# One later slot for the filler work of a hybrid decoder step on one core

## The chip, the cores and the metric

The kernel runs on one core of one Trainium2 chip, in one launch. The metric is the time of an execution on the device in microseconds (us); a median of several runs is compared. The engines are called as in the profile: PE (TensorE, the matmuls), PEld (its weight loads), DVE (VectorE), ACT (ScalarE), POOL (GpSimd) and SP (SyncE, which here only issues DMAs). A small q behind a name (SPq, ACTq) is that engine's sequencer issuing a DMA.

## The reference, cut to what matters

One layer of a decoder trunk, for 1024 prompt tokens and 8 sample tokens that share the weights:

```python
h = rmsnorm(x, norm_gain)
q, k, v, gla_g, a_lr, u, pool_g, xq, xg, merge = split(h @ w_in)
o, S   = gla_chunked(q, k, v, log_sigmoid(a_lr @ w_a2 + b_a) / 16, S0)   # gated linear attention, 4 heads
p      = multiscale_pool(u, history, pool_w, pool_scale)                  # trailing means 2/4/8/16
c      = cross_attn(xq, mem_k, mem_v)                                     # 4 heads, 256 memory rows
b      = [rmsnorm(o) * silu(gla_g), p * silu(pool_g), c * silu(xg)]
merged = sum(sigmoid(merge[n]) * (b[n] @ w_branch[n]) for n in range(3))
y      = rmsnorm(x + merged @ w_out, final_gain)
```

The prompt's memory keys and values are themselves products of the memory rows; the sample tokens have their own cached keys, values, GLA states and pooling rows. All of it is float32 in and out. Outputs are y for both groups, the new keys and values, GLA states and pooling rows.

## The kernel before

**Precision.** A float32 product is made of three fast ones: each operand is split into a high part (`h`, by ACT) and a low part (`l`, by DVE), and PE adds high·high, low·high and high·low. In the profile these three are the lines L242 to L244 (`mm3`), the splits L223 and L224 (`split`), or L226 and L227 where a factor is applied as well (the queries, 1/16).

**The backbone.** The input projection `h @ w_in` is cut into 36 pairs of column blocks. Each pair is made of seven products instead of eight (a Strassen-like scheme; the left operands `a11`, `a12`, `s2`, `s1`, `s3`, `s4`, `a22` of `Pair.operands`), each product runs in two halves of 258 columns, 12 matmuls each. Such a half is called a slot here: 36 × 14 = 504 slots. `prepare` splits the left operands three products ahead, and loads the next pair's weights (`raw`, 512 KB each, two per pair, L296) on ACT's DMA queue right behind one of its splits.

**The filler.** Everything between the projection and the branch products is laid into the slots. `fill` (called once after each slot) advances generators: `cross_steps` (cross-attention) and behind it `gla_steps` (GLA), chained by `mix`; then `pool_steps`. A generator yields a number of units after each step; `Stream.run` runs steps as long as the units done are below 493 · (slot − 28) / 329 for `mix`, so a slot is worth 1.4985 units. `pool_steps` starts once `mix` is over, and has its own rate from slot 357 on. So the yields alone say how many slots of backbone matmuls lie between two steps. The sample tokens' own generators (`cross_sample`, `gla_sample`) are advanced from inside `cross_steps` and `gla_steps`.

**Order.** The kernel writes out PE's and SP's order by hand: PE and SP execute in the order of the code. DVE, ACT and POOL are ordered by a scheduler, which arranges them anew when PE's order changes; each then works strictly in its order. The small psum tiles `pz` of the filler have two buffers, the `px` of the backbone six. The four buffers called `own` (function `V`) hold the sample tokens' data, among them in `gla_sample` two states `s` (L674) and two broadcast value rows `vb` (L1036) at a time.

**The places that the change and the prediction touch.** (Line numbers are those of the kernel before; in the changed kernel those after L861 are one lower.)

- Start of `cross_steps`: `cross_memory(0)` and `cross_queries(0, 0)` split keys and queries (`mkT`, `xqs`/`xq`), `cross_rows(0)` turns the sample queries to rows (PE L753, ACT L755) and stores them, then the first `cross_scores` (`pz<-mkTh,xqsh` and the like).
- `gla_sample`, per head: states are updated in L1042 (ACT) and L1043 (DVE), multiplied on PE in L1060, the result is scaled by its norm in L1069 (ACT) and turned over in L1075 (PE).
- `gla_steps`: gates of the next chunk (PE L919, then a long row of DVE work L903 to L947), `gla_within` (PE L956 to L958, then DVE L959 and the split into `ak`), `gla_recur` (PE `pz<-vsh,ak`).
- First step of `pool_steps` for a group: PE L1139 and L1142, DVE L1145 (`f`) and L1146 (`ds`); second step: loads, window sums and PE L1207, which reads `ds`.

Of the kernel before, what the change touches and what calls it, by code (L numbers as in the profile page):

```python
# [24 lines left out]
NH = 4  # L25
# [22 lines left out]
def trunk_kernel(ctx: ExitStack, tc: tile.TileContext,  # L48
# [185 lines left out]
    def split_in(x, shape, name, scale=None):  # L234

        hi, lo = R(shape, F32R, name + "h"), x.bitcast(F32R)
        split(hi, lo, x, scale)
        return hi, lo
# [447 lines left out]
    def cross_load(h):  # L686
        cross["raw", h] = [loaded(mkv_scr[o][h], [2, DV], "mkv") for o in range(2)]

    def cross_memory(h):
        mk, mv = cross["raw", h]  # L690
        t = PZ()
        for i in range(2):
            for a in range(2):
                nc.tensor.transpose(t[:, i * NM + a * P:i * NM + (a + 1) * P], mk[:, a, i * P:(i + 1) * P], ident)
        cross["mk", h] = split_r(t.rearrange("p (i m) -> p i m", i=2), [2, NM], "mkT")
        cross["mv", h] = split_in(mv, [2, DV], "mvs")

    def cross_fetch(h, c):
        cross["xq", h, c] = loaded(chunk_of(xq_raw[h], c), [2, CT], "xq")

    def cross_queries(h, c):
        cross["q", h, c] = split_in(cross["xq", h, c], [2, CT], "xqs", 1.0 / 16.0)

    def cross_scores(h, c):
        xh, xl = cross["q", h, c]
        mh, ml = cross["mk", h]
        t = PZ()
        for j in range(2):
            for i in range(2):
                cs = slice(j * P, (j + 1) * P)  # L710
                mm3(t[:, j * NM:(j + 1) * NM], xh[:, i, cs], xl[:, i, cs], mh[:, i], ml[:, i], i == 0, i == 1)
        nm = tiny(2, "nm")
        nc.vector.tensor_reduce(nm, t.rearrange("p (j m) -> p j m", j=2), axis=AX.X, op=ALU.max, negate=True)
        p = R([2, NM], name="p")
        sm = tiny(2, "sm")
        for j in range(2):
            act(p[:, j], t[:, j * NM:(j + 1) * NM], AF.Exp, bias=nm[:, j:j + 1], accum_out=sm[:, j:j + 1])
        nc.vector.reciprocal(sm, sm)
        for j in range(2):
            nc.vector.tensor_scalar(p[:, j], p[:, j], sm[:, j:j + 1], None, op0=ALU.mult)  # L720
        cross["p", h, c] = p

    def cross_weights(h, c):
        p = cross["p", h, c]
        t = PZ()
        for a in range(2):
            for j in range(2):
                nc.tensor.transpose(t[:, (2 * a + j) * P:(2 * a + j + 1) * P], p[:, j, a * P:(a + 1) * P], ident)  # L728
        cross["pT", h, c] = split_r(t.rearrange("p (a t) -> p a t", a=2), [2, CT], "pT")
# [105 lines left out]
    def cross_steps():  # L835
        def scores(n):
            cross_scores(n // 4, n % 4)

        def memory(n):
            if n % 4 == 0:  # L840
                cross_memory(n // 4)

        def weights(n):
            cross_weights(n // 4, n % 4)

        def values(n):
            cross_values(n // 4, n % 4)

        samples = chain_of(cross_sample(h) for h in range(NH))
        cross_load(0)  # L850
        cross_fetch(0, 0)
        cross_fetch(0, 1)
        yield 1.5
        cross_memory(0)
        cross_queries(0, 0)
        yield 1.5
        cross_scaled(0)
        cross_rows(0)
        yield 1
        for s in range(16 + 2):  # L860
            if s < 16:  # L861
                scores(s)
                if s == 0:
                    cross_queries(0, 1)
                yield 3
                if 0 < s < 15:
                    cross_queries(*divmod(s + 1, 4))
                if s + 2 < 16:
                    cross_fetch(*divmod(s + 2, 4))
            if s % 4 == 2 and s < 14:  # L870
                cross_load(s // 4 + 1)
            if s == 0:
                cross_keys(0, 0)
                cross_keys(0, 1)
            if s >= 1:
                yield next(samples, 0)
            if 0 <= s - 2:
                values(s - 2)
                yield 1.7
            if s >= 1:  # L880
                yield next(samples, 0)
            if s % 4 == 3 and s < 15:
                memory(s + 1)
                yield 2
            if 0 <= s - 1 < 16:
                weights(s - 1)
                yield 1.7
            for _ in range(3):
                if s >= 1:
                    yield next(samples, 0)  # L890
        yield from samples

    def chain_of(gens):
        for g in gens:
            yield from g
# [122 lines left out]
    def gla_sample(h):  # L1018
# [48 lines left out]
        r = rstd_of(sq, 1.0 / DV)  # L1067
        for i in range(2):
            nc.scalar.activation(os_[:, i], os_[:, i], AF.Copy, scale=r[:, i:i + 1])  # L1069
        yield 1  # L1070
        yield 0.5
        t = PZ()
        for i in range(2):
# [157 lines left out]
    def mix():  # L1231
        yield from cross_steps()
        yield from gla_steps()
# [344 lines left out]
```

## Time and profile before

| | |
|---|---|
| median of 3 runs | 1435.47 us (1434.07 to 1435.5) |
| the profiled execution | 1435.0 us, its span 1433.3 us |
| PE busy | 1413.6 us, 99% of the span |
| DVE busy | 916.5 us, 64% |
| ACT busy | 679.4 us, 47% |
| POOL busy | 220.0 us, 15% |
| chain that ended last | PE 93%, DVE 3%, DMA 2%, ACT 1%, issue 1% |
| mean granted PE clock | 0.998 |

The first table of a profile page gives busy time per engine; the chain of what ended last says on which engine the end of the program hung. Both say PE here, nearly without holes. What is to be read beyond that are the holes: the view of waits lists for each engine who ended its idle times, the timeline shows single instructions with the idle time before them in brackets, and the windows view gives the granted clock of a stretch, 1.00 being 2.4 GHz and 0.50 being 1.2 GHz.

### The profile page before, as it was taken

To read this page: it belongs to the slowest core of one execution; us is meant where nothing else is said; L and a number is where in the kernel's file an instruction comes from. 1 tells how busy PE (TensorE), PEld (TensorE's weight loads), DVE (VectorE), ACT (ScalarE), POOL (GpSimd) and SP (SyncE) were. 2 spreads that over 40 slices of the span, in tenths; PEclk is the share of its full clock that TensorE was granted. 3 is DMA by queue.
4 is the path that set the end of the run, shared out by engine and by line. 5 is a ranking of instruction groups with operands and counts; after the bars stand their busy time and mean duration, and the time that the engine had idled before them with its cause. 6 is when DMAs were issued, how large, how long until landed. Compare 5 with 4: busy or idle time off the path is not lost.

```text
span 1433.3 us, 28230 instructions
## 1 busy us (share of the span) xinstructions
PE 1413.6 (99%) x10689; PEld 1354.0 (94%) x10689; DVE 916.5 (64%) x2123; ACT 679.4 (47%) x1575; POOL 220.0 (15%) x401
## 2 busy tenths in 40 slices
PE   7999999999999999999999999999999999999998
PEld 6899999999999998999999999999999999999876
DVE  6956666766777767867765868775672534554336
ACT  6744544444566655656644545444471422333222
POOL 3212111124432212121221111110010000000000
PEclk9999999999999999999999999999999999999999
DMA  9357575666655554555554546566484687632633
GB/s 332 125 165 230 195 254 163 221 211 169 163 163 156 158 173 141 165 157 160 163 152 153 170 154 193 168 206 205 141 278 144 226 265 257 219 103 84 220 120 116
DMA packets 185812, 259.43 MB, mean 181 GB/s; under 512 B 22460, under 2 KB 136916, under 8 KB 185668
## 3 DMA queue, kind: packets, MB, share of 16 engines
q1 hardware_dynamic: 124188, 146.11, 32.8%
q0 software_dynamic: 23328, 73.56, 14.7%
q10 hardware_dynamic: 38160, 37.95, 9.4%
q8 instruction: 84, 1.38, 0.4%
q14 instruction: 52, 0.43, 0.1%
HBM read 180.47 MB, written 77.56 MB: 180 GB/s over the span
## 4 chain that ended last, share of the span: by engine, by line
PE 93%; DVE 3%; DMA 2%; ACT 1%; issue 1%; DVEq 0%; SPq 0%; ACTq 0%
PE px L242 27%; PE px L243 26%; PE px L244 26%; PE pz L244 3%; PE pz L242 3%; PE pz L243 3%; DMA raw<-in_w_in_dram 2%; PE pz L975 1%; PE pz L408 1%; PE pz L956 1%; PE pz L809 1%; PE pz L958 1%; PE pz L728 0%; PE pz L919 0%; DVE ot L224 0%
## 5 line engine op out<-in xcount | busy, mean ns | idle before, releaser
L243 PE MATMUL px<-bl,wbh 128*128 128x384 f32 (+1 forms) x576 | 184.1, 320 | 0.0
L244 PE MATMUL px<-bh,wbl 128*128 128x384 f32 (+1 forms) x576 | 184.1, 320 | 0.0
L242 PE MATMUL px<-bh,wbh 128*128 128x384 f32 (+1 forms) x576 | 183.7, 319 | 0.0
L558 ACT ACTIVATE r<-px 128x258 f32<-128x258 f32 x240 | 90.4, 377 | 63.4 <-PE px L244 62.9
L242 PEld LDWEIGHTS px<-bh,wbh 128*128 128x128 f32 x576 | 108.4, 188 | 0.0
L243 PEld LDWEIGHTS px<-bl,wbh 128*128 128x128 f32 x576 | 108.2, 188 | 0.0
L244 PEld LDWEIGHTS px<-bh,wbl 128*128 128x128 f32 x576 | 108.2, 188 | 0.0
L242 PE MATMUL px<-o,a11h 128*128 128x258 f32 x320 | 94.0, 294 | 0.0
L242 PE MATMUL px<-ot,s3h 128*128 128x258 f32 x320 | 93.3, 292 | 0.1
L242 PE MATMUL px<-ot,s1h 128*128 128x258 f32 x320 | 93.1, 291 | 0.0
L242 PE MATMUL px<-ot,a22h 128*128 128x258 f32 x320 | 92.9, 290 | 0.0
L242 PE MATMUL px<-o,s4h 128*128 128x258 f32 x320 | 92.5, 289 | 0.2 <-DVE c L640 0.2
L242 PE MATMUL px<-o,a12h 128*128 128x258 f32 x320 | 92.5, 289 | 0.0
L242 PE MATMUL px<-ot,s2h 128*128 128x258 f32 x320 | 92.5, 289 | 0.0
L243 PE MATMUL px<-o,a11h 128*128 128x258 f32 x320 | 91.7, 287 | 0.3 <-DVE o L224 0.3
L244 PE MATMUL px<-o,a11l 128*128 128x258 f32 x320 | 91.1, 285 | 0.0
L243 PE MATMUL px<-ot,s2h 128*128 128x258 f32 x320 | 90.1, 282 | 0.5 <-DVE ot L224 0.5
L243 PE MATMUL px<-ot,a22h 128*128 128x258 f32 x320 | 90.6, 283 | 0.0
L243 PE MATMUL px<-o,a12h 128*128 128x258 f32 x320 | 90.4, 283 | 0.0
L244 PE MATMUL px<-o,a12l 128*128 128x258 f32 x320 | 90.4, 283 | 0.0
L244 PE MATMUL px<-ot,s3l 128*128 128x258 f32 x320 | 90.4, 283 | 0.0
L243 PE MATMUL px<-ot,s1h 128*128 128x258 f32 x320 | 90.3, 282 | 0.0
(471 smaller groups left out, 4626.9 us busy)
## 6 DMA issues: line engine op xcount, KB each, us to landing
raw<-in_w_in_dram ACTq DMA_DIRECT2D x72, 512.0 KB, 4.0
msc<-c POOLq DMA_DIRECT2D x24, 516.0 KB, 4.6
brsc<-c POOLq DMA_DIRECT2D x24, 516.0 KB, 3.8
sig<-msc SPq DMA_DIRECT2D x24, 516.0 KB, 6.2
brr<-brsc SPq DMA_DIRECT2D x48, 256.0 KB, 5.0
wbr<-in_w_branch_dram SPq DMA_DIRECT2D x24, 512.0 KB, 5.5
acc<-sig POOLq DMA_DIRECT2D x16, 516.0 KB, 5.6
acc<-acc SPq DMA_DIRECT2D x16, 516.0 KB, 6.8
```

The source lines that it names most:

```text
L242: nc.tensor.matmul(out, lhsT=lh, rhs=rh, start=start, stop=False, skip_group_check=more)
L243: nc.tensor.matmul(out, lhsT=lh, rhs=rl, start=False, stop=False, skip_group_check=more)
L244: nc.tensor.matmul(out, lhsT=ll, rhs=rh, start=False, stop=stop, skip_group_check=more)
L408: nc.tensor.matmul(t[:, :DV], lhsT=memT[k // 2][:, k % 2, a * P:(a + 1) * P], rhs=raw[k // 2][:, k % 2], start=k == 0, stop=k == NK - 1)
L558: nc.scalar.activation(r, acc[c][:, :QT], AF.Copy)
L809: nc.tensor.matmul(t[32 * j:32 * j + 32, :DV], lhsT=pm[:, a, 4 * i + j, :], rhs=vc[j][:, a, :], start=a == 0, stop=a == 1)
L956: nc.tensor.matmul(t[0:64, 0:P], lhsT=ki[:, 0:64], rhs=qi, start=True, stop=True)
L958: nc.tensor.transpose(t[:, P:2 * P], kt, ident)
L975: nc.tensor.matmul(to, lhsT=kiqi[:, 1, cs], rhs=st, start=False, stop=True)
```

## The change

```diff
@@ cross_steps
         yield 1.5
         cross_scaled(0)
         cross_rows(0)
-        yield 1
+        cross_queries(0, 1)
+        yield 2.5
         for s in range(16 + 2):
             if s < 16:
                 scores(s)
-                if s == 0:
-                    cross_queries(0, 1)
                 yield 3
@@ gla_sample
         for i in range(2):
             nc.scalar.activation(os_[:, i], os_[:, i], AF.Copy, scale=r[:, i:i + 1])
-        yield 1
+        yield 1 if h + 1 < NH else 2.5
         yield 0.5
```

No instruction is added or removed. The split of the second block of queries is issued ahead of the first scores, and 1.5 units more stand behind the rows; 1.5 units more stand behind the scaling of the last head's samples. Counted through the units of the 300 steps of `mix`: the first three stay in their slots (29, 30, 31), the next 295 stand exactly one slot later, and the last two stand two slots later. The first step of `pool_steps` moves from slot 359 to slot 361; its second step was in slot 361 and stays there, and so do all others of the pooling.

Place one is the start of the cross stage. On DVE before (L227 splits a block of queries, L713 takes the maximum of scores, L623 is an eviction of the backbone, L718 and L720 end a softmax):

```order
L224 TENSOR_TENSOR mkv<-mkv,mvsh 128x512
L227 SCALAR_TENSOR_TENSOR xq<-xq,xqsh 128x512
L623 TENSOR_TENSOR c_1519<-px,r_1403 128x258
L305 TENSOR_TENSOR ws<-raw 128x512
L713 TENSOR_REDUCE nm<-pz 128x2
L623 TENSOR_TENSOR c_1519<-px,r_1417 128x258
L718 RECIPROCAL sm<-sm 128x2
L720 TENSOR_SCALAR p<-p,sm 128x256 x2
L227 SCALAR_TENSOR_TENSOR xq<-xq,xqsh 128x512
```

and now:

```order
L224 TENSOR_TENSOR mkv<-mkv,mvsh 128x512
L227 SCALAR_TENSOR_TENSOR xq<-xq,xqsh 128x512
L623 TENSOR_TENSOR c_1519<-px,r_1403 128x258
L227 SCALAR_TENSOR_TENSOR xq<-xq,xqsh 128x512
L623 TENSOR_TENSOR c_1519<-px,r_1417 128x258
L224 TENSOR_TENSOR a11l<-raw,a11h 128x512
L713 TENSOR_REDUCE nm<-pz 128x2
```

The second split has moved from behind the first softmax to ahead of the first maximum. On PE the twelve matmuls of one backbone slot now stand between L753 and the first scores, where nothing stood.

Place two is in GLA, around the third L1060 (head 1, first half of the samples). On PE before (`a22` and `a12` are backbone products):

```order
L242 MATMUL px<-ot_986,a22h 128x258
L243 MATMUL px<-ot_987,a22h 128x258
L244 MATMUL px<-ot_986,a22l 128x258
L1060 MATMUL pz<-s_6915,pm 32x256 x2
L1060 MATMUL pz<-s_6919,pm 32x256 x2
L242 MATMUL px<-o_497,a12h 128x258
```

and now (L1059 is the old L1060):

```order
L242 MATMUL px<-o_501,a12h 128x258
L243 MATMUL px<-o_502,a12h 128x258
L244 MATMUL px<-o_501,a12l 128x258
L1059 MATMUL pz<-s_6932,pm 32x256 x2
L1059 MATMUL pz<-s_6936,pm 32x256 x2
L242 MATMUL px<-o_497,a12h 128x258
```

The states' product stands behind the first half of `a12` instead of ahead of it, as everything of GLA stands one slot later against the backbone. On DVE just behind this place, before (L1043 reads `vb`, `ws<-raw` and `a11l` read backbone weights, L903 to L923 are GLA gates):

```order
L224 TENSOR_TENSOR s3l<-ws,s3h 128x512
L623 TENSOR_TENSOR c_7343<-px,r_7204 128x258
L623 TENSOR_TENSOR c_7343<-px,r_7223 128x258
L1043 SCALAR_TENSOR_TENSOR s_7361<-vb,smp,s_7361 128x256
L224 TENSOR_TENSOR a11l<-raw,a11h 128x512
L903 TENSOR_SCALAR bz<-pz,vec 128x256
L305 TENSOR_TENSOR ws<-raw 128x512
L906 TENSOR_TENSOR bz<-bz 128x256
L1043 SCALAR_TENSOR_TENSOR s_7361<-vb,smp,s_7361 128x256
L923 SCALAR_TENSOR_TENSOR bz<-smask,bz 128x256
```

and now (L1042 is the old L1043, L902, L905 and L922 the old L903, L906 and L923):

```order
L623 TENSOR_TENSOR c_7336<-px,r_7218 128x258
L224 TENSOR_TENSOR a11l<-raw,a11h 128x512
L1042 SCALAR_TENSOR_TENSOR s_7370<-vb,smp,s_7370 128x256
L305 TENSOR_TENSOR ws<-raw 128x512
L1042 SCALAR_TENSOR_TENSOR s_7374<-vb,smp,s_7374 128x256
L902 TENSOR_SCALAR bz<-pz,vec 128x256
L1042 SCALAR_TENSOR_TENSOR s_7374<-vb,smp,s_7374 128x256
L905 TENSOR_TENSOR bz<-bz 128x256
L922 SCALAR_TENSOR_TENSOR bz<-smask,bz 128x256
```

The two backbone instructions `a11l` and `ws<-raw` have moved from behind the first L1043 of the second pair of states to ahead of it.

Place three is the start of the pooling. On PE before (`s3` and `a11` are backbone products):

```order
L244 MATMUL px<-ot_817,s3l 128x258
L1139 MATMUL pz<-sel,hist 128x8 x2
L1142 MATMUL pz<-ident,smp 8x128 x2
L242 MATMUL px<-ot_812,s3h 128x258
L243 MATMUL px<-ot_813,s3h 128x258
```

and now (lines one lower):

```order
L244 MATMUL px<-o_429,a11l 128x258
L1138 MATMUL pz<-sel,hist 128x8 x2
L1141 MATMUL pz<-ident,smp 8x128 x2
L1206 MATMUL pz<-ds,pwr 128x8 x4
L242 MATMUL px<-o_421,a11h 128x258
```

The product that reads `ds` (old L1207) stood 24 backbone matmuls behind L1142 and now stands directly behind it. On DVE the two instructions that make `ds` had an eviction between them before:

```order
L1077 TENSOR_SCALAR brs_120<-pz,vec 128x8 x2
L1145 TENSOR_TENSOR f_10457<-pz,smp 128x16
L640 TENSOR_TENSOR c_10272<-px,r_10437 128x258
L1146 SCALAR_TENSOR_TENSOR ds<-f_10457,smp 128x16
L224 TENSOR_TENSOR a12l<-raw,a12h 128x512
```

and now follow each other:

```order
L1076 TENSOR_SCALAR brs_120<-pz,vec 128x8 x2
L640 TENSOR_TENSOR c_10267<-px,r_10445 128x258
L224 TENSOR_TENSOR a12l<-raw,a12h 128x512
L1144 TENSOR_TENSOR f_10495<-pz,smp 128x16
L1145 SCALAR_TENSOR_TENSOR ds<-f_10495,smp 128x16
```

`a12l` and the eviction stand ahead of both.

## Rows read from the trace of the kernel before

**Rows 1.** Waits of PE, whole run (who ended it: us, times, longest us).

```profile
PE pz L956 <- DVE ak L224: 2.4, 1, 2.4
PE pz L1075 <- ACT os L1069: 1.0, 1, 1.0
...
PE pz L244 <- DVE xq L227: 0.7, 2, 0.5
...
PE pz L242 <- ACT xqsh L226: 0.3, 1, 0.3
```

**Rows 2.** Timeline, start of the cross stage (start us, us, instruction, [idle before]).

```profile
122.12 0.39 PE L753 MATMUL pz<-ident,xsq 128*8 128x128 f32 x2
...
122.81 0.38 PE L242 MATMUL pz<-mkTh,xqsh 128*128 128x256 f32 x1 [0.30 <-ACT xqsh L226]
...
123.05 0.68 DVE L227 SCALAR_TENSOR_TENSOR xq<-xq,xqsh 128x512 fp32r<-128x512 f32 x1
...
123.79 0.38 PE L244 MATMUL pz<-mkTh,xq 128*128 128x256 f32 x1 [0.48 <-DVE xq L227]
```

**Rows 3.** Timeline, last GLA samples and first pooling step.

```profile
738.35 0.28 PE L244 MATMUL px<-ot,s1l 128*128 128x258 f32 x1
...
739.63 0.83 PE L1075 MATMUL pz<-ident,os 128*128 128x128 f32 x4 [1.00 <-ACT os L1069]
...
740.22 0.37 PE L242 MATMUL px<-ot,s3h 128*128 128x258 f32 x1
...
741.76 0.51 PE L1139 MATMUL pz<-sel,hist 120*128 120x8 f32 x4
...
742.13 0.38 PE L1142 MATMUL pz<-ident,smp 128*8 128x128 f32 x2
742.26 0.36 PE L242 MATMUL px<-ot,s3h 128*128 128x258 f32 x1
...
742.55 0.17 DVE L1145 TENSOR_TENSOR f<-pz,smp 128x16 f32<-128x16 f32 x1 [1.68 <-PE pz L1142]
...
742.97 0.17 DVE L1146 SCALAR_TENSOR_TENSOR ds<-f,smp 128x16 f32<-128x16 f32 x1
```

**Rows 4.** Timeline behind the third L1060, up to PE's longest wait.

```profile
523.48 0.38 SPq L1036 DMA_DIRECT2D vb<-vs  x1
523.56 0.39 ACTq L296 DMA_DIRECT2D raw<-in_w_in_dram  x1
...
530.37 0.48 DVE L1043 SCALAR_TENSOR_TENSOR s<-vb,smp,s 128x256 f32<-128x256 f32 x1 [3.37 <-ACT s4h L223]
530.77 0.68 DVE L224 TENSOR_TENSOR a11l<-raw,a11h 128x512 fp32r<-128x512 f32 x1
...
533.03 0.69 DVE L305 TENSOR_TENSOR ws<-raw 128x512 f32<-128x512 f32 x1 [1.18 <-DMA raw<-in_w_in_dram]
...
540.16 0.29 PE L956 MATMUL pz<-kiqi 128*64 128x128 f32 x1 [2.43 <-DVE ak L224]
```

**Rows 5.** DMA issues of 523.4 to 523.9 (count, KB each, us to landing).

```profile
raw<-in_w_in_dram ACTq DMA_DIRECT2D x1, 512.0 KB, 9.4
vb<-vs SPq DMA_DIRECT2D x1, 256.0 KB, 6.8
```

**Rows 6.** DMA issues, whole run (count, KB each, median us).

```profile
raw<-in_w_in_dram ACTq DMA_DIRECT2D x72, 512.0 KB, 4.0
```

**Rows 7.** Windows: stretch, its us, busy of PE, PEld, DVE, ACT, POOL, PEclk.

```profile
540.50:543.90 3.40, 3.40 (x18) 3.37 (x17) 2.12 (x9) 3.27 (x12) 0.00 (x0) 0.50 0.03 5
```

**Rows 8.** Timeline, start of GLA.

```profile
372.23 0.46 SPq L674 DMA_DIRECT2D s<-in_state_gla_dram  x1
...
373.48 0.37 ACTq L296 DMA_DIRECT2D raw<-in_w_in_dram  x1
...
378.42 0.69 DVE L305 TENSOR_TENSOR ws<-raw 128x512 f32<-128x512 f32 x1
...
385.20 0.35 PE L242 MATMUL pz<-vsh,ak 128*128 128x256 f32 x1 [0.24 <-DVE ak L224]
```

## Prediction

> **What bounds the kernel now.** I read the page's busy table and its chain first: PE is busy 99% of the span and carries 93% of the chain, so time can only come out of PE's holes, or out of stretches in which its clock is low. The change neither adds nor removes an instruction; it can only open and close holes. So the next view was the list of who ended PE's waits [rows 1]. Leaving out the first 70 us, which the change does not reach, it is short: one wait of 2.4 us for DVE's split `ak` in GLA, one of 1.0 for the scaling `os` of the last head's samples, and three at the first two score blocks of the cross stage (0.3 for `xqsh`, 0.7 in two waits for `xq`). The timelines of those places came next [rows 2 to 4], then the landing times of the DMAs beside them [rows 5, 6], and last the granted clock behind the longest wait [rows 7]: for 3.4 us behind it PE runs at 0.50, the lower of its two levels, at which it does half of what it would do. The mean of 0.998 over the span leaves 2.9 us lost to the clock in all, of which this stretch is 1.7; a second one like it has no room beside it.
>
> A wait costs a little more than its idle time. At L1075 the start is 1.28 us behind that of the last backbone matmul (738.35 to 739.63) where the usual step is about 0.13 (twelve in 740.22 to 741.76); 1.00 is idle, so 0.15 more is lost when the pipeline starts again [rows 3].
>
> **The change part by part.** The scale is the slot: its twelve matmuls take 1.54 us [rows 3].
>
> *Start of the cross stage.* Before, the first scores follow L753 at once. They stand until ACT has split the queries (0.30) and, at their third matmul, until DVE has made the low part, which ends at 123.05 + 0.68 = 123.73 (0.48) [rows 2]. The remaining 0.2 of the 0.7 is the second block, whose split comes late behind the first softmax. With one slot between, the first scores come at about 122.36 + 1.5 = 123.9 and need the low part 0.25 later, at 124.1, 0.4 behind 123.73. The second block's split is now done ahead of the first maximum, so its wait goes too. The split holds up one eviction of the backbone by 0.6 us on DVE; the six `px` buffers cover that. Together 1.0 of idle time and three restarts of 0.15: −1.4 us. Bounds: −1.4, and 0 if the split still arrives last.
>
> *Scaling of the last samples.* L1075 gets one slot more distance. The scaling came 1.00 late, a slot is 1.54, so the wait goes: −1.15 with its restart. Bounds −1.15 and 0.
>
> *First pooling step.* It moves two slots, the second step none, so L1207 now stands right behind L1142. PE could have gone on at 742.26, the start of its next instruction; instead it must wait for `f` and `ds`. DVE took up `f` at 742.55 and `ds`, with an eviction between them, at 742.97, ending 743.14 [rows 3]. Without the eviction `ds` follows `f` at about 742.73 and ends at 742.90. The wait is 0.64, with its restart +0.8. The loads that these steps read are issued on SP long before PE comes, so no DMA is late here. Behind the waiting PE instruction stands the whole backbone; nothing covers it. Bounds: +0.4 (DVE answers faster than here) and +1.9 (`a12l`, 0.68 as for `a11l` [rows 4], and the eviction, 0.4, are still ahead of `f` when PE is through).
>
> *Everything between, one slot later against the backbone.* Filler steps keep their distances to each other; what shifts is their place against the backbone's splits and weight loads. The place where this matters is the 2.4 us wait. The loads `vb` (SP) and `raw` (ACT's queue) are issued 0.08 us apart [rows 4], and take 6.8 and 9.4 us [rows 5], where the median `raw` takes 4.0 [rows 6]. DVE, in its fixed order, stands until `vb` has landed (530.37), does `a11l`, and stands again 1.18 us until `raw` has landed (533.03); all the GLA gates and the split `ak`, for whose psum buffer PE then waits at 540.16, are queued behind [rows 4]. In the new order `vb` waits for a L1060 that is one slot later, so `raw` goes out some 1.4 us ahead of it, and `a11l` and `ws<-raw` stand ahead of the wait for `vb`. If `raw` then lands before `vb`, three things leave the stretch between the landing of `vb` and `ak`: the wait of 1.18 and two instructions of some 0.6 each (0.68 and 0.69 long, overlapping the next). That is 2.4 of a wait of 2.43. I leave 0.2 of it. And the stretch at half clock goes, worth 3.4 / 2 = 1.7 [rows 7], since no such stretch followed the waits of 1.0 and less. Together −(2.2 + 1.7) = −3.9. Bounds: −4.3 (all of it with its restart), and +0.5 if `vb` comes later by as much, instead.
>
> The Trainium skill speaks against this term. "DMA: Bandwidth & Descriptors", section "Issuing engines are not separate DMA queues", says that transfers started by different engines run on the same 16 DMA engines and interleave, whoever started them. By that rule a lead of 1.4 us on another queue does not take `raw` out of the traffic of `vb`; it would share with it and with the stores beside it all the same. Rows 5 agree in so far as both are slow there at once. What the kernel does if `raw` stays at 9.4 is the first rival.
>
> *Other steps of GLA and of the cross stage* get new neighbours. Only one more shows a wait before, 0.24 at the start of GLA [rows 8]; I count one further wait of this size with its restart, +0.4. Bounds −0.4 (that wait goes and none comes) and +2 (two of the size of L1075's).
>
> Sum: −1.4 − 1.15 + 0.8 − 3.9 + 0.4 = −5.25 us. The profiled execution took 1435.0 us (span 1433.3, 1.7 around it), 0.5 below the median of 1435.47. From the median: 1430.2 us.
>
> **The rivals.**
>
> *`raw` still takes 9.4 us.* Issued 1.4 ahead of `vb`, it lands 9.4 − 1.4 − 6.8 = 1.2 behind `vb`. DVE stands at `ws<-raw` as before, only `a11l` (0.6) is out of the way; PE waits 1.8 and the half clock probably follows again. That term is then −0.6, the sum −1.95, the time 1433.5. For it: on both occasions the same stores are on the way. Against it: the median of 4.0 [rows 6], which says that `raw` is fast unless it comes behind the rest.
>
> *The clash moves to the start of GLA, and the kernel is slower.* There the first load of `s` goes out at 372.23 and `raw` at 373.48; DVE takes up `ws<-raw` at 378.42, and its row of work reaches the `ak` for which PE already stands 0.24 at 385.20 [rows 8]. One slot later, `s` goes out on top of `raw`. If `raw` is then as slow as at 523 (9.4 instead of the 4.9 or less that 378.42 allows), DVE is 4.5 late, PE waits that much more and loses 1.7 in clock behind it: +6.2, in all 1436.4, slower than now. It decides from where `raw` takes over some 8.4 us. Against it: no `vb` is near (the first needs rows that PE turns over only just ahead of 385.20), and `s` alone is a plain load.
>
> *The change doesn't do what it says*: the scores and L1075 wait as before because the splits and scalings are ordered later on ACT and DVE as well. Then 1430.2 + 2.55 = 1432.8. Against it: the order on DVE up to the first low part is the same as before, and 0.4 us are to spare.
>
> **How the numbers follow.** A measurement of this kernel can tell about 0.2%, 2.9 us, from no change: under 1432.6 is faster, over 1438.3 is slower. Chances: the sum as forecast 0.57; `raw` still slow 0.25; the clash at GLA's start 0.10; no effect at the two places 0.08. The forecast's own range is 1428.3 (the wait gone wholly, no new one) to 1432.5 (a pooling wait of 1.9 and one more of 1 us). The first two cases hold 0.82, so the range reaches from 1428.3 to 1434.5. Faster: 0.57 of the forecast, a little of each of the others, 0.62. Slower by over 0.2% needs the clash together with the old wait: 0.08. The rest, 0.30, is within.
>
> **What would show it.** In the list of PE's waits the rows for `xqsh`, `xq` and `os` are gone, and a new one stands there for DVE's `ds` of about 0.6. The wait for `ak` near 540 is under 0.5 us, the load `raw` beside it lands in under 8 us and ahead of `vb`, and no stretch behind it shows a clock of 0.50. Wrong would be: the wait for `ak` still near 2 us with the low clock behind it (first rival), a wait at the start of GLA of over 2 us (second), or a wait of over a microsecond at a place which none of the rows show.

## The result

| | before | changed |
|---|---|---|
| median, runs taken side by side | 1434.44 us (12 runs, 1432.54 to 1435.69) | 1438.43 us (12 runs, 1435.53 to 1441.58) |
| changed / before | | 1.0027, 95% interval 1.0018 to 1.0036 |
| the profiled execution | 1435.0 us, span 1433.3 | 1436.05 us, span 1434.3 |
| PE busy | 1413.6 us | 1412.3 us |

The change costs about 4 us, 0.27%; 5 us less than before had been forecast. The profiled execution of the changed kernel is one of its better ones, 2.4 under its median. A second profile (below, "the changed kernel once more") took 1438.03.

Who ended PE's waits from 70 to 1400 us in the changed kernel (engine, what it waits with, who ended it, total us, times, longest); this answers to [rows 1]:

```profile
engine line waited for: us in total, times, longest us
PE pz L955 <- DVE ak L224: 3.1, 2, 1.6
PE pz L242 <- DVE pTl L224: 1.2, 1, 1.2
PE pz L243 <- DVE dfl L224: 0.9, 1, 0.9
PE pz L242 <- ACT dfh L223: 0.8, 1, 0.8
PE pz L1206 <- PE pz L1141: 0.5, 1, 0.5
PE pz L1059 <- PE px L244: 0.3, 1, 0.3
PE px L242 <- DVE c L640: 0.2, 1, 0.2
```

The three waits that were to go (`xqsh`, `xq`, `os`) are gone. In their place stand one for `pTl` (the low part of the turned-over softmax weights), two for `ak` where there was one, and three where the pooling starts: together 7.0 us of idle time after 70 us, where the same view of before adds up to 4.8. The list of waits sees only part of it: each wait also costs 0.15 to 0.25 at the restart, and in some executions a stretch at half clock.

On PE's timeline (start, duration, engine, line, instruction, idle time before it in brackets), the waits are these:

```profile
312.24 0.39 PE L242 MATMUL pz<-mkTh,xqsh 128*128 128x256 f32 x1 [1.21 <-DVE pTl L224]
...
448.68 0.29 PE L955 MATMUL pz<-kiqi 128*64 128x128 f32 x1 [1.50 <-DVE ak L224]
...
541.71 0.29 PE L955 MATMUL pz<-kiqi 128*64 128x128 f32 x1 [1.64 <-DVE ak L224]
...
743.62 0.81 PE L1206 MATMUL pz<-ds,pwr 128*128 128x8 f32 x6 [0.52 <-PE pz L1141]
...
751.26 0.38 PE L242 MATMUL pz<-dfh,pwh 128*128 128x256 f32 x1 [0.77 <-ACT dfh L223]
...
752.53 0.38 PE L243 MATMUL pz<-dfl,pwh 128*128 128x256 f32 x1 [0.88 <-DVE dfl L224]
```

The profile names L1141 as releaser of L1206; what L1206 reads last is `ds`, which DVE ends at 743.34 + 0.17 = 743.51.

What DVE does ahead of three of these waits (same columns; DVE works strictly in this order):

```profile
306.04 0.71 DVE L591 STREAM_TRANSPOSE vt<-c 128x512 f32<-128x512 f32 x1
310.06 0.42 DVE L772 CUSTOM_DVE_ANT_0 kc<-kc,qb 128x256 f32<-128x256 f32 x1 [3.31 <-DMA raw<-in_w_in_dram]
...
311.50 0.69 DVE L224 TENSOR_TENSOR pTl<-pz,pTh 128x512 fp32r<-128x512 f32 x1
...
440.60 0.49 DVE L1042 SCALAR_TENSOR_TENSOR s<-vb,smp,s 128x256 f32<-128x256 f32 x1 [3.42 <-ACT r L558]
...
533.72 0.48 DVE L1042 SCALAR_TENSOR_TENSOR s<-vb,smp,s 128x256 f32<-128x256 f32 x1 [3.62 <-DMA vb<-vs]
```

Each time DVE stands for over 3 us at an instruction on the sample tokens' data, and what PE needs next (`pTl`, or the GLA gates that lead to `ak`) is queued behind. The releasers named at 310 and 440 are not the cause: L772 does not read `raw`, nor L1042 `r`. Of the loads that they do read, the trace has `qb` issued at 303.74 and landed after 6.09 us, 0.23 ahead of L772; `vb` issued at 436.75 and 526.68 and landed after 3.73 and 6.91 us, 0.12 and 0.13 ahead of L1042. At 533 the states `s` came hardly sooner: they landed at 532.95, and ACT, which scales them ahead of L1042, took them up at 533.03. Whether these loads were the cause, the experiments had to tell.

At the pooling start, DVE of the changed kernel:

```profile
744.69 0.36 DVE L1209 TENSOR_SCALAR brs<-pz,vec 128x8 f32<-128x8 f32 x2 [1.17 <-PE pz L1206]
746.78 0.69 DVE L224 TENSOR_TENSOR s2l<-ws,s2h 128x512 fp32r<-128x512 f32 x1 [1.73 <-ACT s2h L223]
747.51 0.69 DVE L305 TENSOR_TENSOR ws<-raw,ws 128x512 f32<-128x512 f32 x1
748.12 0.43 DVE L1176 TENSOR_TENSOR sw<-u 128x271 f32<-128x271 f32 x1
...
751.79 0.68 DVE L224 TENSOR_TENSOR dfl<-df,dfh 128x512 fp32r<-128x512 f32 x1
```

and of the kernel before:

```profile
745.47 0.43 DVE L1177 TENSOR_TENSOR sw<-u 128x271 f32<-128x271 f32 x1
...
748.31 0.69 DVE L224 TENSOR_TENSOR s2l<-ws,s2h 128x512 fp32r<-128x512 f32 x1 [0.40 <-ACT s2h L223]
...
749.64 0.68 DVE L224 TENSOR_TENSOR dfl<-df,dfh 128x512 fp32r<-128x512 f32 x1
```

Before, the window sums (`sw`, then `df`, whose split PE needs as `dfh` and `dfl`) ran ahead of `s2l`, in time in which DVE would have stood. Now they are queued behind `s2l` and its wait of 1.73, and start 2.65 later, while their matmuls have kept their slot.

### The profile page after: what moved, and what is told of

The parts are those of the page before. It is cut to its first block, busy times and chain, and to the rows that moved or that the text cites. A ratio compares the mean times of both kernels' runs of the same rounds, so it can differ in the third digit from the quotient of the medians.

```text
span 1434.3 us, 28229 instructions
## 1 busy us (share of the span) xinstructions
PE 1412.3 (98%) x10689; PEld 1352.9 (94%) x10689; DVE 914.2 (64%) x2123; ACT 679.8 (47%) x1575; POOL 222.5 (16%) x401
## 4 chain that ended last, share of the span: by engine, by line
PE 93%; DVE 3%; DMA 2%; ACT 1%; issue 1%; SPq 0%; DVEq 0%; ACTq 0%
PE px L242 26%; PE px L243 26%; PE px L244 26%; PE pz L243 3%; PE pz L242 3%; PE pz L244 3%; DMA raw<-in_w_in_dram 1%; PE pz L408 1%; PE pz L974 1%; PE pz L955 1%; PE pz L809 1%; PE pz L957 1%; DVE ot L224 0%; DMA s<-in_state_gla_dram 0%; PE pz L728 0%
## 5 line engine op out<-in xcount | busy, mean ns | idle before, releaser
L244 PE MATMUL px<-ot,s1l 128*128 128x258 f32 x320 | 90.4, 283 | 0.0
```

The source lines that it names most:

```text
L244: nc.tensor.matmul(out, lhsT=ll, rhs=rh, start=False, stop=stop, skip_group_check=more)
```

## The experiments

All times are medians; each was compared with runs of the kernel before on the same chip (1434.2 to 1434.9 us), and the ratio is that to the kernel before, with its 95% interval. A difference to the changed kernel compares two such ratios, which were taken on different occasions. "Pooling steps 360/361" are the slots of the first and second step of `pool_steps`; before they are 359/361, in the changed kernel 361/361.

**The new start alone, held in its old slots.** 299 of 300 filler steps unmoved, pooling 359/361.

```diff
+        cross_queries(0, 1)
-        yield 1
+        yield 2.5
...
-                if s == 0:
-                    cross_queries(0, 1)
-                yield 3
+                yield 3 if s else 1.5
```

> The second queries go ahead of the first scores and one slot stands behind the rows, as in the changed kernel, but the 1.5 units are taken back behind the first scores: 299 of the 300 filler steps keep their old slots, and the scaling of the last samples is left alone. Theory (the one-slot shift of all of GLA and most of the cross stage costs the time): the waits for xqsh and xq are gone, the waits for pTl near 311 and for ak near 447 don't appear, the old wait of 2.4 near 540 stays; 1.4 us below the kernel before, with its narrow spread of about 3 us. Rival 1 (the loss sits at the start of the pooling): the same here, -1.4. Rival 2 (the new start itself does the harm, by what it does to DVE at 122 us): 1 to 4 us above the kernel before.

Measured: 1434.77, ratio 1.0005 (0.9992 to 1.0017). The waits for `xqsh` and `xq` are gone, none stands near 311 or 447, that of 2.4 near 540 stays. But the 1.4 did not arrive, which neither the theory nor a rival had said. The runs spread over 8.2 us, and so did those of the kernel before beside them, over 7.6. In its profile, the longest of its runs, PE waits 1.3 near 148, where the profile of before shows no wait, and 2.3 near 641 behind a `raw` that took 7.8 us to land, with half clock after it.

**The first part of the change alone.** 297 steps one slot later, pooling 360/361.

```diff
+        cross_queries(0, 1)
-        yield 1
+        yield 2.5
...
-                if s == 0:
-                    cross_queries(0, 1)
```

> The first part of the change alone: 297 steps one slot later, the last samples' scaling as before, the first pooling step one slot ahead of the second. Theory (the shift costs): the waits for pTl near 311 (1.2) and for ak near 447 and 540 (1.5 and 1.6) stand there as in the changed kernel, the runs spread over 5 us or more, and the time is 1 to 4 us above the kernel before. Rival 1 (the pooling start): at most a small wait near 743, and the time is 1 to 1.5 us below the kernel before, since only the waits at 122 are gone.

Measured: 1437.13, ratio 1.0017 (1.0006 to 1.0028). Waits for `pTl` 1.4, for `ak` 1.5 and 1.0, as the theory had it, but also waits for `dfh` and `dfl` (1.0 and 0.8), which neither had forecast with a slot between the two pooling steps. The wait for `os` is gone without the second part of the change.

**The second part alone.** 298 steps unmoved, pooling 360/361.

```diff
-        yield 1
+        yield 1 if h + 1 < NH else 2.5
```

> The second part of the change alone: 298 steps in their old slots, the last two one slot later, the first pooling step one slot ahead of the second. Theory (the shift costs): the wait of 1.0 for os is gone, at the pooling start there may be a wait of up to 0.6, the rest is as before: 0.5 to 1.2 us below the kernel before, spread about 3 us. Rival 1 (the pooling start): waits of 0.8 and 0.9 for the splits of the pooled samples stand there as in the changed kernel, and the time is 1 us above the kernel before or more.

Measured: 1432.41, ratio 0.9986 (0.9977 to 0.9996): faster. It has no wait for `os` and none at the pooling start, against the rival; its profile, the longest of its runs (1438.9), has others of 0.9 near 387 and 2.0 near 663. The two parts alone give +0.17% and -0.14%; together they give +0.27%. They hinder each other.

**Both distances, both held.** As the first experiment, with the second part, and the last head's final units left out; pooling 359/361.

```diff
-        yield 1.2
+        if h + 1 < NH:
+            yield 1.2
```

> Both distances are opened and both are taken back at once: 1.5 units less behind the first scores, and the last head's final 1.2 units left out, so that the shift of a slot and the crowding at the pooling start are both gone. Theory (the shift costs): -1.4 and -1.15, 2.5 us below the kernel before (about 0.17%), spread about 3 us. Rival 1 (the pooling start): the same. Rival 2 (the new start does the harm itself): above the kernel before.

Measured: 1433.65, ratio 0.9993 (0.9984 to 1.0002). That is 0.9 below the kernel before, where 2.5 had been expected; a wait of 1.9 stands near 148 in its profile.

**The shift in the cross stage alone.** The first part of the change, and 1.5 units taken back in GLA's first step; pooling 359/361.

```diff
         gla_values(0, 0)
-        yield 5
+        yield 3.5
```

> The first part of the change, but the 1.5 units are taken back in the first step of GLA: only steps 4 to 140, all of the cross stage, stand one slot later; GLA and the pooling keep their old slots. Theory (the shift lets waits of DVE for sample data stand ahead of what PE needs, in both stages): the waits at 122 are gone (-1.5), the wait for pTl near 311 is there (+1.4 to 1.5), none for ak near 447, the old one of 2.4 near 540: within 1 us of the kernel before. Rival 1 (the loss sits in GLA or at the pooling start alone): no wait near 311, 1.4 us below. Rival 2 (the new start does the harm itself, at 122 to 150): 2 us or more above, with waits near 148.

Measured: 1435.82, ratio 1.0010 (1.0000 to 1.0020), 1.2 above the kernel before, where at most 1 had been expected. PE waits 1.3 for `pTl` and 2.5 for `ak` near 540, and not near 447, as the theory had it. Its profile, one of its longest runs, has four more waits of 0.3 to 0.6 that the profile of before doesn't have, and one near 387 that has grown from 0.2 to 0.6.

**The shift in GLA alone.** The start of before, `yield 6.5` in GLA's first step; pooling 360/361.

```diff
         gla_values(0, 0)
-        yield 5
+        yield 6.5
```

> The start of the kernel before, and 1.5 units more in the first step of GLA: only steps 141 to 300, all of GLA, stand one slot later, and the first pooling step one slot ahead of the second. Theory: the waits at 122 stay, none near 311, the wait for ak near 447 (1.5) and those for dfh and dfl near 751 (0.9 and 0.9) are there, the one near 540 falls from 2.4 to 1.0 to 1.6: 1 to 3 us above the kernel before. Rival (the shift of GLA is harmless, the cross stage carries the loss): within 1 us of the kernel before.

Measured: 1434.45, ratio 0.9997 (0.9989 to 1.0006), spread 2.5 us. The number is the rival's. There is no wait near 311; those for `ak` are 0.5 near 447, where 1.5 had been expected, and 0.7 near 540; those for `dfh` and `dfl` are 1.0 and 0.8, and the one for `os` is gone. What the shift takes at the pooling start it gives back at 540.

**The changed kernel with a later pooling.** Pooling 361/363, later steps two slots later.

```diff
-Stream(pool_steps(), WORK_B, int(14 * 25.5), 14 * 36 - 6)
+Stream(pool_steps(), WORK_B, int(14 * 25.5) + 2, 14 * 36 - 4)
```

> The changed kernel with the second and all later pooling steps two slots later, so that the first and the second have their two slots of distance again. Rival 1 (the pooling start is the main cost): the waits for ds, dfh and dfl near 743 to 752 are gone (0.5, 0.8, 0.9 and their restarts, 2.8 in all), 2.5 to 3 us below the changed kernel, about 1 above the kernel before. Theory (the shift through both stages is the main cost): 1 us or less below the changed kernel, 3 above the kernel before, and the waits near 311, 447 and 540 as in the changed kernel.

Measured: 1433.21, ratio 0.9995 (0.9986 to 1.0004): 0.32% under the changed kernel. PE's waits in its profile, from 70 to 1400 us:

```profile
PE pz L955 <- DVE ak L224: 2.7, 2, 1.5
PE pz L242 <- DVE pTl L224: 1.8, 1, 1.8
PE pz L1059 <- PE px L244: 0.4, 1, 0.4
PE px L242 <- DVE c L640: 0.2, 1, 0.2
```

Of the list only the three waits at the pooling start have gone. The rival wins against the theory, which allowed 1 us: taking the pooling start away is worth 5.2 by the medians, more than the 2.8 of its rows.

**The changed kernel once more.**

> The changed kernel once more, for a second profile of it. Theory: the waits for pTl near 311 and ak near 447 come back within 0.3 us of 1.2 and 1.5, since the order on DVE is fixed; where the time is above 1437, further waits of PE stand at places where DVE waited for a load, and a stretch of 3.4 us at half clock behind one of them. Rival 2 (the extra time lies somewhere else than in PE's waits, in slower matmuls or in the start and end): the same waits, and the rest is not in the list.

Measured: 1438.03 (one run). `pTl` 1.84 near 312, `ak` 1.50 near 449 and 0.86 near 542, `ds`, `dfh`, `dfl` 0.52, 0.77 and 0.89, to 0.01 as before; further 0.25 near 215 and 0.50 near 443. No half clock between 70 and 1400. The places of the waits came back; their sizes, where a load decides, vary, that for `pTl` by more than the 0.3 allowed. Of the two reasons given for a time above 1437, the further waits were there and the half clock was not.

**The kernel before with an early pooling.** Filler untouched, pooling 359/359.

```diff
-Stream(pool_steps(), WORK_B, int(14 * 25.5), 14 * 36 - 6)
+Stream(pool_steps(), WORK_B, int(14 * 25.5) - 2, 14 * 36 - 8)
```

> The kernel before with its 300 filler steps untouched, and the second and later pooling steps two slots earlier, so that the first and the second share a slot as in the changed kernel. If the pooling start carries the loss by itself (the theory now): waits for ds (0.5) and for dfh and dfl (0.8 and 0.9) appear near 743 to 752, a stretch at half clock behind them in part of the executions, 2.5 to 4.5 us above the kernel before. If it costs only together with the shifted GLA: less than 1 us above.

Measured: 1435.92, ratio 1.0007 (0.9998 to 1.0017). `ds` 0.7 and `dfl` 0.4, no wait for `dfh`; half clock for 3.4 us from 742.9. That is about 1 us, between the two expectations: two steps in one slot cost less where GLA stands in its old slots.

**The changed kernel, pooling one slot later** (361/362; `+ 1` and `- 5` in the same place).

> The changed kernel with the second and later pooling steps one slot later: the second then stands where it stood before with respect to all of GLA but its last two steps, and one slot behind the first. If the place of the windows against the end of GLA decides: no wait for ds, dfh or dfl, 3 to 5 us below the changed kernel, as with two slots. If two slots between the first and the second step are needed: the waits for dfh and dfl stay, as where only the start was shifted, and the time is 0.5 to 1.5 us below the changed kernel.

Measured: 1434.39, ratio 0.9997 (0.9989 to 1.0006), 0.30% under the changed kernel. `ds` and `dfh` gone, `dfl` 0.3. One slot does nearly what two do: the place of the second step against the end of GLA decides. Two earlier runs say the same: the scaling alone and GLA shifted alone both have their pooling steps in 360/361, and only the second, with GLA a slot later, waits for `dfh` and `dfl`.

**GLA shifted alone, pooling later** (`yield 6.5`, and `+ 2`, `- 4`; pooling 360/363).

> GLA one slot later with the cross stage as before, and the pooling from its second step two slots later. The waits for dfh and dfl (2.2 with their restarts) are gone against the kernel with GLA shifted alone: 2 to 3 us below that one and below the kernel before, 1431.5 to 1432.5. If the pooling start costs only in the changed kernel: no difference to GLA shifted alone.

Measured: 1431.48 (1430.33 to 1432.92), ratio 0.9979 (0.9970 to 0.9988). Its waits:

```profile
PE pz L956 <- DVE ak L224: 1.1, 2, 0.6
PE pz L244 <- DVE xq L227: 0.7, 2, 0.5
PE px L242 <- DVE c L640: 0.5, 2, 0.3
PE pz L242 <- ACT xqsh L226: 0.3, 1, 0.3
PE pz L1060 <- PE px L244: 0.3, 1, 0.3
```

In all 11 runs the mean clock is 0.999 or more. This kernel beats both the one before and the changed one, with no part of the change in it as it was written.

**The same with the new start, held** (`yield 3 if s else 1.5` as well).

> The early second queries and the slot behind the rows with the cross stage's other steps in their old slots, GLA one slot later, the pooling from its second step two slots later. Sum of the parts: waits at 122 gone (-1.5), the one for os (-1.2), that at 385 (-0.5), the one near 540 shorter (-1 to -1.8, and its half clock gone), against it waits near 447 and 561 (+0.7 to +2.2 together): 2.5 to 4 us below the kernel before, 1430.5 to 1432. If the waits at 122 come back later as one near 148 in most executions: 1432 to 1433.5.

Measured: 1431.33 (1428.98 to 1432.42), ratio 0.9975 (0.9964 to 0.9985), not told apart from the one before. The waits at 122 are gone, and one stands near 148. DVE and PE there:

```profile
146.34 0.43 DVE L772 CUSTOM_DVE_ANT_0 kc<-kc,qb 128x256 f32<-128x256 f32 x1 [2.96 <-DMA vc<-in_cache_mem_v_dram]
...
149.06 0.42 DVE L649 TENSOR_TENSOR c<-px,r 128x258 f32<-128x258 f32 x1
...
149.53 0.39 PE L242 MATMUL px<-o,a12h 128*128 128x258 f32 x1 [1.48 <-DVE c L649]
```

PE comes earlier, DVE stands at L772 for a load, and the eviction `c` is queued behind: the 1.5 saved at 122 are waited for at 148. The three held starts show 1.3, 1.9 and 1.5 there. That is no new cost of the start: the run with the scaling alone, whose start is that of before, shows 0.65 there, and DVE of the kernel before stood nearly as long at the same product (2.57 against 2.96), only that PE did not come so early:

```profile
145.35 0.42 DVE L772 CUSTOM_DVE_ANT_0 kc<-kc,qb 128x256 f32<-128x256 f32 x1 [2.57 <-DMA qb<-xqs]
...
308.90 0.42 DVE L772 CUSTOM_DVE_ANT_0 kc<-kc,qb 128x256 f32<-128x256 f32 x1 [1.13 <-DMA qb<-xqs]
```

The second of these rows of before is the product ahead of `pTl`.

**Which loads?** The next four are the changed kernel with one thing taken away. First, the second half of the key and query-row loads.

```diff
-            kcs, qb = cross["kc", h, b // 2]
+            kcs, qb = cross["kc", h, b // 2 % 2]
...
-            if b in (1, 3):
-                cross_keys(h, b // 2 + 2)
```

> The changed kernel, but the sample tokens' third and fourth pair of cached keys and of query rows per head are not loaded: their products are made with the first two pairs, so these scores are others than the reference's. If the wait for pTl near 311 comes from DVE standing for these late loads: that wait (1.2 to 1.8) is gone, DVE's idle stretch of 3 us ahead of it too, and the time is 1.5 to 2.5 us below the changed kernel, 1436 to 1437. If pTl is late by its own input: the wait stays.

Measured: 1436.59, ratio 1.0017 (1.0008 to 1.0026), but the wait for `pTl` is 1.49 and DVE's idle stretch ahead of L772 still 3.30. The wrong loads: those issued from 303 to 306 are a head's first two pairs, and they had stayed in; `qb` of the first, issued at 304.25, landed after 6.1 us, 0.2 ahead of L772. This expectation failed. Its profile shows something else, the granted clock in three windows (us, busy time of each engine and its instructions, clock, DMA) behind `dfh` and `dfl`:

```profile
core 0: us, PE busy (x) PEld busy (x) DVE busy (x) ACT busy (x) POOL busy (x), PEclk, DMA share, GB/s
748.00:752.00 4.00, 2.34 (x18) 1.94 (x17) 3.96 (x13) 1.54 (x3) 0.00 (x0) 1.00 0.15 35
752.00:755.40 3.40, 3.40 (x16) 3.40 (x17) 2.23 (x5) 0.63 (x1) 0.00 (x0) 0.50 0.32 84
755.40:758.00 2.60, 2.60 (x23) 2.60 (x23) 0.73 (x2) 1.61 (x4) 0.00 (x0) 1.00 0.69 194
```

Here the pooling start costs 1.7 us more (3.4 at half clock), with the same waits as in the two profiles of the changed kernel, which have no such stretch; the profile of the first part alone has it too, from 753.3.

**No value rows** (`vb`).

```diff
-            vb = V([2, DV], name="vb")
-            nc.sync.dma_start(out=vb, in_=v_scr[h][b0:b0 + 2].partition_broadcast(P))
-            return s0, vb
+            return s0, s0
```

> The changed kernel, but the sample states of GLA are updated with themselves and not with the broadcast value rows, which are not loaded; the states and their outputs are others than the reference's. If the waits for ak near 447 and 540 come from DVE standing for vb: they are gone or under 0.5 (1.5 and 0.9 to 1.6 before), the one near 561 may go with them, and the time is 2.5 to 4 us below the changed kernel, 1434.5 to 1436. If DVE stands there for the states s or for raw: the waits stay above 1.

Measured: 1432.78, ratio 0.9990 (0.9979 to 1.0001), 0.37% under the changed kernel, more than expected:

```profile
PE pz L242 <- DVE pTl L224: 1.6, 2, 1.4
PE pz L243 <- DVE dfl L224: 0.9, 1, 0.9
PE pz L242 <- ACT dfh L223: 0.8, 1, 0.8
PE pz L1204 <- PE pz L1139: 0.5, 1, 0.5
PE px L242 <- DVE c L640: 0.2, 1, 0.2
```

Both waits for `ak` and the one for L1059 are gone, and that for `pTl` stays. With `vb` gone the states `s` have more buffers and are loaded earlier too, so that the run shows the pair of loads, not `vb` by itself.

**No query rows** (`qb`).

```diff
-        qb = [wk.tile([P, DV], F32, tag=t, name="qb", bufs=2) for t in ("alc", "st")]
-        for bb in range(2):
-            nc.sync.dma_start(out=qb[bb], in_=xq_scr[h][2 * b2 + bb].partition_broadcast(P))
-        cross["kc", h, b2] = kc, qb
+        cross["kc", h, b2] = kc, [k[:, 0] for k in kc]
...
-  tensor_tensor_reduce(kc[:, a, :], kc[:, a, :], qb[b % 2],
+  tensor_tensor_reduce(kc[:, a, :], kc[:, a, :], kc[:, a, :],
```

> The changed kernel, but the sample tokens' query rows qb are not loaded and the cached keys are multiplied with themselves; these scores are others than the reference's. In the run before, the loads that DVE stands for near 310 turned out to be those of a head's first pair (qb landed 6.1 after its issue, 0.2 ahead of L772), and they had stayed in. If qb is what DVE stands for: its wait ahead of the products near 310 is shorter by 1 or more, PE's wait for pTl (1.2 to 1.8) is under 0.5, and the time is 1 to 2.5 us below the changed kernel. If the keys kc land as late: both waits stay.

Measured: 1434.40, ratio 0.9990 (0.9976 to 1.0005), 0.37% under the changed kernel, which again is more than the expected 1 to 2.5 us. PE doesn't wait for `pTl`, and DVE does not stand there:

```profile
305.88 0.42 DVE L640 TENSOR_TENSOR c<-px,r 128x258 f32<-128x258 f32 x1
306.27 0.43 DVE L769 CUSTOM_DVE_ANT_0 kc<-kc 128x256 f32<-128x256 f32 x1
...
309.10 0.69 DVE L224 TENSOR_TENSOR pTl<-pz,pTh 128x512 fp32r<-128x512 f32 x1
```

**Products off the row.**

```diff
-  tensor_tensor_reduce(kc[:, a, :], kc[:, a, :], qb[b % 2],
+  tensor_tensor_reduce(zeros, zeros, zeros,
```

> The changed kernel with all its loads, but the products of the sample tokens' keys and queries on DVE read a resident tile of zeros (128 columns instead of 256), so they wait for no load and are arranged at the start of the program; these scores are others than the reference's. If a product that waits for its load is what holds pTl up: PE's wait near 311 is gone, and the time is 1.5 us or more below the changed kernel. If pTl is late by ACT or by PE's own work: the wait stays.

Measured: 1439.30, ratio 1.0030 (1.0014 to 1.0046). The wait near 311 is gone, but the time isn't lower: the products, which now wait for nothing, were arranged at the program's start, where the first backbone matmul comes at 32.3 instead of 26.5. From there to the end its profile takes 1.5 less than that of the changed kernel. Only the first half of the expectation came.

## Why the prediction was wrong

**Start of the cross stage: right in its place, -1.5.** Three idle times of 0.30, 0.48 and 0.18 with restarts are gone. Held in the old slots, the same edit gains nothing that can be measured (ratio 1.0005); all three profiles of held starts have a wait near 148 of 1.3 to 1.9.

**Scaling of the last samples: right, -1.15, but for another reason as well.** The wait for `os` goes too where GLA is shifted without the edit (GLA shifted alone, the first part alone). In the changed kernel the edit was no longer needed, and pushed the first pooling step into the second's slot.

**First pooling step: the wait that it named was right, the step behind it was overlooked.** `ds` costs 0.52 and 0.24 at the restart, forecast 0.64 and 0.15. But the sum priced the first step against the second and not the second against GLA, which had moved up to it: the window sums went behind `s2l`, and `dfh` and `dfl` cost 2.07 with their restarts, in some executions 1.7 more in clock. That is 2.8 by the rows; +0.8 was forecast, and 1.9 as its upper bound. This is the first of the two failed steps. Against the same kernel with the pooling one or two slots later (ratios 0.9997 and 0.9995) the pooling start costs 0.30 to 0.32%, some 4.5 us. What the rest above 2.8 is stays open. The half clock is not the main part of it: the 5 of the changed kernel's 12 runs with a mean clock of 0.999 have a median of 1437.36, the 8 such runs with the pooling two slots later 1432.95. These lie 4.4 apart, where all runs of the two lie 5.2 apart.

**The wait for `ak` at 540: the chain was right, its size was not.** `raw` does go out ahead, at 524.20, lands after 4.1 us and is no longer waited for. From the landing of `vb` to PE's restart it takes 8.12 instead of 9.88, 1.8 less where 2.2 had been forecast. But `vb`, issued at 526.68, took 6.9 us, as in [rows 5], DVE stood 3.62 for it, and PE came 13.4 behind its issue where it had come 14.2 behind. So PE's wait fell by 0.8 (1.6 in the second profile) and not by 2.2. The two loads in question, in the window from 526 to 527.5 of the changed kernel (name, queue, count, KB each, us to landing):

```profile
s<-in_state_gla_dram SPq DMA_DIRECT2D x1, 256.0 KB, 6.7
vb<-vs SPq DMA_DIRECT2D x1, 256.0 KB, 6.9
```

The lead of `raw` took nothing off `vb`: `raw` had landed at 528.29, 5.3 ahead of `vb`, and `vb` took as long as before, beside the load of `s` and three stores `onsc` of POOL (5.5). This fits the rule from the Trainium skill that the prediction weighed ("DMA: Bandwidth & Descriptors", section "Issuing engines are not separate DMA queues"), by which transfers interleave whoever started them; no run here shows more of it.

The half clock behind the wait is gone in both profiles of the changed kernel, as forecast. But its 1.7 us were probably not in every execution of before: of its 34 runs beside the first four experiments, 19 have a mean clock of 0.999 or more, and the profile with that stretch has 0.998. By that count the median holds less than the 1.7 that was subtracted from it. That is a reading of mean clocks, not of 34 traces, and the five profiles of other kernels that keep GLA in its old slots show the stretch in four.

**Everything else, one slot later: the second failed step.** It was put at +0.4 with an upper bound of +2. The waits that came are 1.21 for `pTl`, 1.50 for `ak` near 447 and 0.32 at L1059, 3.5 with their restarts (4.1 and a further 1.2 near 215 and 443 in the second profile); 0.24 at 385 went, 0.49 with its restart. I had looked for places that already waited in the trace of before. What matters is where DVE stood without PE noticing: at 308.90 it waited for `qb` in the kernel before too, with the split that PE needs still in time. For `pTl` the mechanism is shown: `qb` lands 0.23 ahead of the product that DVE stands at, and without `qb` the wait is gone. For `ak` it is shown for `vb` and `s` together: without `vb` the waits are gone, but `s` came earlier in that run too. The shift of GLA alone is not enough near 447: in all three profiles in which GLA stands a slot later and the cross stage doesn't, the wait is 0.51, and in all eight in which both do and `vb` is loaded it is 1.33 to 1.52. Why, stays open.

In the profile of the changed kernel the terms are then, restarts included: -1.5 (122), -1.2 (`os`), -0.5 (385), -0.8 at 540 and -1.7 for its clock, +3.5, +2.8: +0.6, where the spans differ by 1.0. The other 0.4 stands at 1362, in eight small matmuls of the output product. Their rows in the kernel before, the changed kernel and its second profile:

```profile
1361.85 1.06 PE L1498 MATMUL px<-wos,mgs 128*32 128x512 f32 x8
...
1362.48 1.43 PE L1497 MATMUL px<-wos,mgs 128*32 128x512 f32 x8
...
1363.82 1.96 PE L1497 MATMUL px<-wos,mgs 128*32 128x512 f32 x8
```

None of the other fifteen kernels loses time there, and the cause is open. The program's end is the same: PE's last matmul starts 6.86 us ahead of the end of the span before and 6.89 ahead of it now, and the clock falls only behind it (to 0.50 from 1431.3 and from 1430.9).

The second profile, 0.4 under the median, stands for a typical execution. Its span is 3.0 longer than that of before, and the same sum gives -1.5, -1.2, -0.5, -1.6 at 540, -1.7 for the clock, +4.1, +1.2, +2.8, +0.9 at 1362 and +0.3 ahead of the filler: +2.8, without any half clock of its own. Against an execution of before that lacks the stretch at half clock the difference is 4.7. The 4 us between the medians lie between the two.

Runs with one thing taken away don't add up like this. The later pooling, the value rows and the query rows are each worth 0.32 to 0.37%, more than the whole change costs, where the rows of the first profile show 2.8, 3.9 and 1.4 us. So they show that each of these takes part, not which is the largest.

None of the rivals was it: `raw` was not slow at 524, the start of GLA did not clash, and the change did what it says. The last sign of being wrong that the prediction named came true: waits of over a microsecond at places which none of its rows show. Two smaller things: the forecast started from 1435.47, the median of three runs, where twelve gave 1434.44; and the bounds of its terms add up to 1428.6 as the lower end, not 1428.3.

## What to carry to other kernels

When filler work is moved as a block, price its two ends and not only its inside: what stays in place (here the second pooling step) is met by what moved. In an order fixed in advance, look in the trace of before for every long idle time of the in-order engine that ends with a load, even where nobody waited: that is where a shifted order turns a hidden wait into an open one. And undo the parts one by one: one half of this change was worth 2 us, and a single yield elsewhere, with the pooling moved along, 3.

## What had not been expected of the hardware

Waits set by work between engines repeat to 0.01 us from one execution to the next (`ds` 0.52, `dfl` 0.88 and 0.89). That for `ak` at 540, which hangs on loads, was 2.42 to 2.45 in five profiles of kernels with GLA in its old slots and 2.07 in a sixth; that for `pTl` varied from 1.21 to 1.84 in the same order. And the clock does not follow the wait alone: the same waits of 0.77 and 0.88 or 0.89 were followed by 3.4 us at 0.50 in one profile and by none in four others. The five waits of 2.42 to 2.45 near 540 all had such a stretch behind them and the one of 2.07 had none, but a wait of 0.73 at the pooling start had one in that same profile, and a wait of 1.96 that ended at 664.76, in the run with the scaling alone, was followed by none either.
